# A hybrid decoder block on one core: the first half's input projection takes the input times the norm's weight alone, and the norm's factor is multiplied onto its results

## Chip, cores and metric

The kernel runs on one core of a Trainium2 chip. The metric is device time in microseconds (us): 2113.87 us, the median of three runs (2112.77 to 2115.74). A core has five engines with one instruction stream each: TensorE (PE, matrix products), VectorE (DVE), ScalarE (ACT), GpSimd (POOL) and SyncE (SP, which issues the DMAs). Each works through its own stream in order and waits on semaphores for the others.

## The reference

One layer on x of 2048 positions by 1024 features, in float32:

```python
h = rmsnorm(x, norm1_g)              # x * rsqrt(mean(x*x) + 1e-6) * g
proj = h @ w_in                      # 3088 columns
p_q, p_k, p_v, p_g, p_a, c_b, c_c, c_h = split(proj)
q, k, v = heads of p_q * 64**-0.5, p_k, p_v
log_a = log_sigmoid(p_a @ w_gate_up + b_gate) / 16
o = rmsnorm(gla_chunked(q, k, v, log_a), gla_norm_g) * silu(p_g)
u = c_c * c_h
o_conv = c_b * causal_depthwise_conv(u, conv_w)      # width 3
x = x + concat(o, o_conv) @ w_out
h2 = rmsnorm(x, norm2_g)
x = x + (silu(h2 @ w_ffn_gate) * (h2 @ w_ffn_up)) @ w_ffn_down
out = rmsnorm(x, norm_f_g)
```

The norm's factor, rsqrt(mean(x*x) + 1e-6), is one number for each position. The norm's weight g is one number for each feature.

## The kernel before

**Layout.** Features lie on the 128 partitions, positions along the free dimension. A tile is 128 features by 512 positions (256 KB). The 2048 positions are four blocks of 512; two blocks (j = 0, 1) make a half, and the input projection, the output projection and the feed-forward part run once for each half. The input comes twice: `xt` as tiles with the features on the partitions, and `x` as rows, from which the squares of the norm are summed.

**Numbers.** Products are made from float32 values that are split in two parts, a high part (an ACT copy that rounds, line 153) and the rest (a DVE subtraction, line 154). Each product of two tiles takes three matmuls: high times high, high times rest, rest times high (lines 366 to 368; in the first unit lines 297 to 299).

**Units.** The input projection of a half (`in_proj`, line 596) has twelve units of 256 columns: k, q, v, v, g, g, then twice the three of the convolution (c_c, c_h, c_b). An ordinary unit (`unit`, line 370) is a Strassen-like scheme with seven products of 12 matmuls in the place of eight. It needs sums and differences of the weight's quarters, which POOL makes (lines 349 to 356) and ACT and DVE split into a buffer of four (`wqp`), and differences T1 to T4 of the operand tiles, which POOL makes for the first half (line 310). Three of its four results end in SBUF through ACT copies and DVE additions (lines 386, 390), the fourth stays in PSUM. The first two units of the first half are plain products of eight parts (96 matmuls each): the first in `build_first` (line 273), so that it can begin before all operands are there, the second in `plain_unit` (line 315).

**The start.** `first_loads` (line 466) issues on SP's queue: four tiles of rows of block 0 (`xr`), two quarters of the first weights, four tiles of `xt`, the other two quarters, four more tiles of `xt`; then the rows and the tiles of block 1. At most eight loads are under way at a time. ACT squares and sums the rows (`row_squares`, line 463), `rows_rstd` (line 449) works out the factor in steps on 128x4 values, and DVE spreads it into `rep` tiles (line 457; two buffers), which PE transposes into a PSUM bank (line 458). `scaled` (line 489) then multiplies each tile of the input by the weight and that bank in one DVE instruction (line 490). The product goes through the split and the six matmuls of its step in the first unit. Block 1's factor follows after the first eight steps.

**Order of the work.** The instructions of each engine are put in order when the program is built, by a scheduler with a timeline of its own, and are then fixed. Work in the background runs between products: `tick` (line 201) calls a step of a list of generators, one after the other: the gate's weights (`gate_weights`, line 494), the factors of blocks 2 and 3 (`row_stats`, line 427), the forget gate of the first half (`gate`, line 547), then `h1_ahead` (line 516), which makes the second half's operands with the same `scaled` and stores them, and later the attention (`gla_half`, line 649). Results of the projection are stored to scratch in DRAM: k, q and v through `settled` (an ACT copy where they stand in PSUM, line 410), g through `silu` (line 420), the convolution's through the lines 622 to 647.

**Buffers.** Tiles `t` (nine), tiles `b` (eleven), operands `op` (28), PSUM banks (eight).

## Time and profile before

| | |
|---|---|
| median of three runs | 2113.87 us |
| profiled execution: span, first to last instruction | 2109.1 us |
| PE busy | 2033.1 us, 9133 matmuls |
| DVE busy | 1418.4 us |
| ACT busy | 1014.1 us |
| POOL busy | 972.4 us |
| moved by DMA | 464.43 MB |

The profile is of one execution. It gives the time of every instruction, what each engine waited for, and in "windows" the busy time of each engine in a stretch of the span. "x" is a count, and a mean is in ns where a row says so. The tile names in a row are the program's (`op` operand, `wq` weight quarter, `h` input tile, `mm` PSUM bank, `rep` and `rb_ps` the spread factor). One time stands beside the span for the whole run: the median, 4.8 us above the span of the profiled execution.

### The profile page before, as it was taken

Reading aid. Unit: us, or ns where it says so; the run is one execution under the profiler, and the core shown is the slowest. Engines: PE = TensorE matmul, PEld = TensorE weight load, DVE = VectorE, ACT = ScalarE, POOL = GpSimd, SP = SyncE. Lnnn points to the kernel's source line nnn. Section 1 sums busy time; section 2 is a strip of 40 time slices with the busy share of each in tenths; the row PEclk is TensorE's granted clock in tenths of the full one; section 3 lists DMA queues with packets and bytes.
Section 4 is the critical chain, followed back from the end, with each engine's and each line's share of the span. In section 5 each row is a group of like instructions: output and inputs, shape, how many; then the busy total and the mean of one; then the engine's idle time right before and its main releaser. Section 6 shows DMA issues by size and latency. Waiting matters only on the chain.

```text
span 2109.1 us, 26874 instructions
## 1 busy us (share of the span) xinstructions
PE 2033.1 (96%) x9133; PEld 1648.9 (78%) x9133; DVE 1418.4 (67%) x1983; ACT 1014.1 (48%) x1997; POOL 972.4 (46%) x703
## 2 busy tenths in 40 slices
PE   5999999999999999999999999999999989999996
PEld 4778888877888878788888878787888868877775
DVE  7669786549753786788786665554766666665564
ACT  5555455656542356445545443333554554543344
POOL 3436322222102464564464348764645544436774
PEclk9999999999999999999999999999999999999998
DMA  7349485425586872656545687697454535587763
GB/s 277 126 158 318 139 329 164 148 83 164 201 284 235 325 249 100 241 198 221 217 172 220 243 327 272 235 338 296 158 207 179 206 134 190 183 344 281 269 269 110
DMA packets 189241, 464.43 MB, mean 220 GB/s; under 512 B 19824, under 2 KB 65072, under 8 KB 179504
## 3 DMA queue, kind: packets, MB, share of 16 engines
q1 hardware_dynamic: 189104, 462.72, 60.4%
q8 instruction: 72, 1.18, 0.2%
q14 instruction: 65, 0.53, 0.1%
HBM read 297.49 MB, written 165.15 MB: 219 GB/s over the span
## 4 chain that ended last, share of the span: by engine, by line
PE 70%; DVE 8%; DMA 7%; ACT 3%; issue 3%; POOL 2%; SPq 0%; DVEq 0%; ACTq 0%; POOLq 0%
PE mm L366 21%; PE mm L368 21%; PE mm L367 21%; DVE wq L154 2%; DMA op<-shT 1%; DVE so L154 1%; PE mm L794 1%; DVE h L490 1%; PE mm L795 1%; PE mm L797 1%; DVE op L154 1%; DMA sx<-y 1%; ACT wq L153 1%; PE o_ps L718 1%; DMA shT<-so 1%
## 5 line engine op out<-in xcount | busy, mean ns | idle before, releaser
L366 PE MATMUL mm<-op,wq 128*128 128x512 f32 x2499 | 981.3, 395 | 23.8 <-DVE c L390 7.8
L368 PE MATMUL mm<-op,wq 128*128 128x512 f32 x2499 | 966.1, 392 | 12.6 <-DVE wq L154 11.9
L367 PE MATMUL mm<-op,wq 128*128 128x512 f32 x2499 | 976.0, 391 | 0.0
L154 DVE TENSOR_TENSOR wq<-raw,wq 128x512 fp32r<-128x512 f32 (+2 forms) x626 | 527.3, 849 | 329.9 <-ACT wq L153 324.3
L153 ACT ACTIVATE wq<-raw 128x512 fp32r<-128x512 f32 (+2 forms) x626 | 363.6, 587 | 555.8 <-PE mm L368 402.4
L366 PEld LDWEIGHTS mm<-op,wq 128*128 128x128 f32 x2499 | 470.8, 188 | 137.6 <-ACT wq L153 12.3
L368 PEld LDWEIGHTS mm<-op,wq 128*128 128x128 f32 x2499 | 470.5, 188 | 123.5 <-DVE wq L154 24.8
L367 PEld LDWEIGHTS mm<-op,wq 128*128 128x128 f32 x2499 | 471.2, 189 | 96.7 <-issue 1.0
L351 POOL TENSOR_TENSOR raw<-s,raw 128x512 f32<-128x512 f32 (+2 forms) x97 | 127.5, 1314 | 422.2 <-DVE wq L154 402.0
L390 DVE TENSOR_TENSOR c<-mm,c 128x512 f32<-128x512 f32 x267 | 183.0, 686 | 95.7 <-PE mm L368 93.0
L349 POOL TENSOR_TENSOR s<-raw 128x512 f32<-128x512 f32 (+2 forms) x97 | 130.2, 1343 | 216.2 <-DMA raw<-in_wffn_dram 88.8
L356 POOL TENSOR_TENSOR raw<-raw 128x512 f32<-128x512 f32 (+2 forms) x97 | 126.7, 1306 | 135.3 <-DVE wq L154 128.1
L386 ACT ACTIVATE c<-mm 128x512 f32<-128x512 f32 x267 | 154.7, 585 | 38.0 <-PE mm L368 36.8
L776 POOL TENSOR_TENSOR ssx<-ssx,q 128x512 f32<-128x512 f32 x52 | 76.5, 1483 | 156.0 <-ACT q L775 155.8
L350 POOL TENSOR_TENSOR raw<-raw 128x512 f32<-128x512 f32 (+2 forms) x97 | 135.1, 1393 | 4.1
L965 POOL TENSOR_TENSOR y<-c,y 128x512 f32<-128x512 f32 x66 | 98.7, 1499 | 49.0 <-DVE c L390 46.6
L154 DVE TENSOR_TENSOR so<-t,so 128x512 fp32r<-128x512 f32 x100 | 91.2, 918 | 25.9 <-ACT so L153 25.4
L153 ACT ACTIVATE wq<-s 128x512 fp32r<-128x512 f32 (+2 forms) x97 | 56.9, 586 | 93.5 <-PE mm L368 83.3
L794 PE MATMUL mm<-op,wq 128*128 128x512 f32 x256 | 100.9, 395 | 0.0
L795 PE MATMUL mm<-op,wq 128*128 128x512 f32 x256 | 99.8, 390 | 0.0
L154 DVE TENSOR_TENSOR wq<-s,wq 128x512 fp32r<-128x512 f32 (+2 forms) x97 | 84.1, 867 | 15.6 <-ACT wq L153 15.0
L153 ACT ACTIVATE so<-t 128x512 fp32r<-128x512 f32 x100 | 62.5, 627 | 41.8 <-DMA sa_T<-so 16.1
(177 smaller groups left out, 1885.0 us busy)
## 6 DMA issues: line engine op xcount, KB each, us to landing
raw<-in_wffn_dram SPq DMA_DIRECT2D x44, 1024.0 KB, 5.7
sa_T<-so SPq DMA_DIRECT2D x88, 512.0 KB, 5.3
op<-sa_T SPq DMA_DIRECT2D x88, 512.0 KB, 9.2
sa_B<-so SPq DMA_DIRECT2D x69, 512.0 KB, 3.4
op<-sa_B SPq DMA_DIRECT2D x69, 512.0 KB, 9.0
raw<-in_win_dram SPq DMA_DIRECT2D x23, 1024.0 KB, 5.5
raw<-in_wdown_dram SPq DMA_DIRECT2D x24, 768.0 KB, 6.2
sx<-y SPq DMA_DIRECT2D x48, 256.0 KB, 3.2
```

Source lines behind the costliest of these rows:

```text
L153: last_hi[:] = [act.activation(hi, src, AF.Copy)]
L154: return dve.tensor_tensor(lo, src, hi.bitcast(F32), ALU.subtract)
L349: pool.tensor_tensor(s1, a21, a22, ALU.add)
L350: pool.tensor_tensor(a21, a11, a21, ALU.subtract)
L351: pool.tensor_tensor(a11, s1, a11, ALU.subtract)
L356: pool.tensor_tensor(a12, a12, a11, ALU.subtract)
L366: pe.matmul(o[:], wh, xh, start=first and k == 0, stop=False, skip_group_check=True)
L367: pe.matmul(o[:], wh, xl, start=False, stop=False, skip_group_check=True)
L368: return pe.matmul(o[:], wl, xh, start=False, stop=k == n - 1, skip_group_check=True)
L386: act.activation(t[:], o[:], AF.Copy)
L390: dve.tensor_tensor(t[:], o[:], t[:], ALU.add)
L794: pe.matmul(o[e, j][:], wh, m[:, 0, :], start=k == 0, stop=False)
```

## The change

The first half's operands are now the input times the weight g; the factor of the position is left out of them. Since the factor belongs to a position, and positions are columns of every result, it can be multiplied onto the results.

- **Loads.** `first_loads` issues the first weights and the 16 tiles of `xt` first, then the second unit's weights, then all eight tiles of rows. Five of the `xt` tiles lie in tiles `t`, eleven in tiles `b` (before: eight and eight).
- **Operands.** For each tile ACT makes the high part straight from the input with g as its scale, DVE makes the rest in one instruction (input times g less the high part; both tensors in SBUF), and POOL multiplies the tile itself by g in place, for the differences T1 to T4. The 16 instructions of line 490 on DVE and the 16 splits behind them become 16 on DVE and 16 on POOL.
- **Factor.** The squares, the two factors and their transposes come after the first unit in the program's text. ACT copies each factor from PSUM to SBUF (`factors`), and for the results c_c its square (`factors2`).
- **Results.** `factored` multiplies a result by the factor: on POOL where it stands in SBUF, on DVE where it stands in PSUM (which takes the place of the ACT copy). It runs on k, q, v, g and c_c; c_h and c_b have none, since c_c takes the square for both itself and c_h, and the convolution's result is multiplied by the factor once more on POOL for c_b. The forget gate multiplies its 16 rows on DVE on the way out of PSUM.
- The first unit's four results are copied out of PSUM by ACT at once. The waits set by hand (`issue_after` on `los`, on `last_load`) are gone.

The second half, its operands (`h1_ahead`) and all that follows are as before.

```diff
@@ -270,25 +270,23 @@
             put("B22", k, b22)
             yield
 
-    def build_first(quad, w):
+    def build_first(h, w):
 
 
         ops = {b: [] for _, b in PRODUCTS}
-        h, o = {}, {}
+        o, out = {}, []
         quarters = ("A11", "A12"), ("A21", "A22")
-        los = []
         for j in range(2):
             for r in range(2):
                 o[r, j] = bank()
             for k in range(KD):
-                with ExitStack() as stack:
-                    if len(los) > 1:
-                        stack.enter_context(tc.issue_after(los[-2].ins))
-                    h[k, j] = quad(k, j)
+                g = col(C_G1 + k)
                 x = opp.tile([P, 2, PB], F32R, name="op", tag="op")
-                los.append(split(h[k, j][:], x[:, 0, :], x[:, 1, :]))
-                if j == 0 and k >= PT:
-                    row_squares(1, k - PT)
+                act.activation(x[:, 0, :], h[k, j][:], AF.Copy, scale=g)
+                dve.scalar_tensor_tensor(
+                    x[:, 1, :], h[k, j][:], g, x[:, 0, :].bitcast(F32), ALU.mult, ALU.subtract
+                )
+                pool.tensor_scalar(h[k, j][:], h[k, j][:], g, 1.0, ALU.mult, ALU.mult)
                 name = ("B11", "B12")[j] if k < 4 else ("B21", "B22")[j]
                 ops.setdefault(name, []).append(x)
                 c = slice(k % 4 * P, (k % 4 + 1) * P)
@@ -297,8 +295,15 @@
                     pe.matmul(o[r, j][:], q[:, 0, c], x[:, 0, :], start=k == 0, stop=False)
                     pe.matmul(o[r, j][:], q[:, 0, c], x[:, 1, :], start=False, stop=False)
                     pe.matmul(o[r, j][:], q[:, 1, c], x[:, 0, :], start=False, stop=k == KD - 1)
-            if j == 0:
-                rbs[1] = rows_rstd(squares[1])
+            for r in range(2):
+                c = tt("c")
+                act.activation(c[:], o[r, j][:], AF.Copy)
+                out.append((r, j, c, False))
+        for b in range(2):
+            for t in range(PT):
+                row_squares(b, t)
+            factors[b] = tiny.tile([P, PB], F32, name="rb", tag="rb")
+            act.activation(factors[b][:], rows_rstd(squares[b])[:], AF.Copy)
 
         def differences(wanted):
             for n, y, a, b in (
@@ -310,11 +315,10 @@
                     pool.tensor_tensor(yy[:], aa[:], bb[:], ALU.subtract)
                     ops[n].append(split_op(yy[:]))
 
-        return ops, [(r, j, o[r, j], True) for j in range(2) for r in range(2)], differences
-
-    def plain_unit(src, ops):
-
-        raw = raw_weights(src)
+        return ops, out, differences
+
+    def plain_unit(raw, ops):
+
         us, columns = [], (("B11", "B21"), ("B12", "B22"))
         for r, row in enumerate(((0, 1), (3, 2))):
             w = [weight_quarter(raw[:, i, :]) for i in row]
@@ -324,7 +328,7 @@
                     for k in range(4):
                         product_step(o, w[i], ops[n], k, i == 0)
                     tick()
-                us.append((r, j, settled(o, True), False))
+                us.append((r, j, o, True))
         return us
 
     def weight_quarter(src):
@@ -458,7 +462,7 @@
             pe.transpose(rb_ps[:, t * P : (t + 1) * P], rep[:], ident[:])
         return rb_ps
 
-    rbs, raws, first_weights, last_load, rows, squares = {}, {}, {}, [], {}, {}
+    rbs, raws, first_weights, rows, squares, factors, factors2 = {}, {}, {}, {}, {}, {}, {}
 
     def row_squares(b, t):
         act.activation(rows[b, t], rows[b, t], AF.Square, accum_out=squares[b][:, t, 0:1])
@@ -466,6 +470,16 @@
     def first_loads():
 
         raw = rawp.tile([P, 4, PB], F32, name="raw", tag="raw")
+        for j in range(2):
+            for k in range(KD):
+                if j == 0 and k % 4 == 0:
+                    for i in ((0, 3), (1, 2))[k // 4]:
+                        raw_loads.append(load(raw[:, i, :], win[0][:, i, :]))
+                h = raws[k, j] = bt("h") if len(raws) > 4 else tt("h")
+                load(h[:], xt[j, :, k, :])
+        for n, i in (("A11", 0), ("A21", 3), ("A12", 1), ("A22", 2)):
+            first_weights[n] = weight_quarter(raw[:, i, :])
+        second = raw_weights(win[1])
         for b in range(2):
             squares[b] = mtiny.tile([P, PT, 2], F32, name="ssq", tag="ssq")
             for t in range(PT):
@@ -473,18 +487,7 @@
                 rows[b, t] = xr[:]
                 r0 = b * PB + t * P
                 load(xr[:], x[r0 : r0 + P, :])
-            for k in range(KD):
-                if b == 0 and k % 4 == 0:
-                    for i in ((0, 3), (1, 2))[k // 4]:
-                        raw_loads.append(load(raw[:, i, :], win[0][:, i, :]))
-                h = bt("h") if b else tt("h")
-                raws[b, k] = h
-                last_load[:] = [load(h[:], xt[b, :, k, :])]
-        for t in range(PT):
-            row_squares(0, t)
-        rbs[0] = rows_rstd(squares[0])
-        for n, i in (("A11", 0), ("A21", 3), ("A12", 1), ("A22", 2)):
-            first_weights[n] = weight_quarter(raw[:, i, :])
+        return second
 
     def scaled(g, rb, h):
         dve.scalar_tensor_tensor(h[:], h[:], g, rb[:], ALU.mult, ALU.mult)
@@ -505,13 +508,11 @@
         split(r1, low[:, :, 2, :], low[:, :, 3, :])
         yield
 
-    def build_h():
-
-
-        def quad(k, j):
-            return scaled(col(C_G1 + k), rbs[j], raws[j, k])
-
-        return build_first(quad, first_weights)
+    def factored(c, in_psum, f):
+
+        s = tt("n") if in_psum else c
+        (dve if in_psum else pool).tensor_tensor(s[:], c[:], f[:], ALU.mult)
+        return s
 
     def h1_ahead():
 
@@ -560,7 +561,12 @@
                         stop=n == "B22" and k == 3 and e == 1, skip_group_check=True,
                     )
         a_sb = bt("a_sb")
-        act.activation(a_sb[:], a[:], AF.Copy)
+        if half:
+            act.activation(a_sb[:], a[:], AF.Copy)
+        else:
+            for j in range(2):
+                r = slice(32 * j, 32 * j + 32)
+                dve.tensor_tensor(a_sb[r, :], a[r, :], factors[j][r, :], ALU.mult)
         yield
         for j in range(2):
             small = decays[2 * half + j] = [
@@ -593,16 +599,20 @@
         dve.tensor_tensor(dn[:, i, :], em[:, i, :], el[:, i, :], ALU.mult)
         store(s_d[b][i][:], t2[:])
 
-    def in_proj(half, ops, first=None, differences=None):
+    def in_proj(half, ops, first=None, second=None, differences=None):
+        def values(u):
+            f = factors2 if u in (6, 9) else factors
+            for r, j, c, p in next(units):
+                if half == 0 and u not in (7, 8, 10, 11):
+                    c, p = factored(c, p, f[j]), False
+                yield r, j, c, p
+
         def units():
             for u in range(12):
-                with ExitStack() as stack:
-                    if half == 0 and u == 1:
-                        stack.enter_context(tc.issue_after(last_load[0].ins))
-                    if half or u > 1:
-                        us = unit(win[u], ops)
-                    else:
-                        us = plain_unit(win[u], ops) if u else first
+                if half or u > 1:
+                    us = unit(win[u], ops)
+                else:
+                    us = plain_unit(second, ops) if u else first
                 if half == 0 and u == 1:
                     del ops["B12"]
                     differences(("T4",))
@@ -611,16 +621,21 @@
         units = units()
         if half == 0:
             differences(("T1", "T2", "T3"))
-        for dst, i0 in ((s_kq, 0), (s_kq, 2), (s_v, 0), (s_v, 2)):
-            for r, j, c, p in next(units):
+        for u, (dst, i0) in enumerate(((s_kq, 0), (s_kq, 2), (s_v, 0), (s_v, 2))):
+            for r, j, c, p in values(u):
                 store(dst[2 * half + j][i0 + r][:], settled(c, p)[:])
         for i0 in (0, 2):
-            for r, j, c, p in next(units):
+            for r, j, c, p in values(4 + i0 // 2):
                 store(s_g[2 * half + j][i0 + r][:], silu(c, p)[:])
         background.append(gla_half(half))
+        if half == 0:
+            for j in range(2):
+                factors2[j] = tiny.tile([P, PB], F32, name=f"rr{j}", tag=f"ssx{j}", bufs=1)
+                act.activation(factors2[j][:], factors[j][:], AF.Square)
         for i0 in (0, 2):
-            cc = {(r, j): settled(c, p) for r, j, c, p in next(units)}
-            ch = {(r, j): c for r, j, c, _ in next(units)}
+            u = 6 + 3 * (i0 // 2)
+            cc = {(r, j): settled(c, p) for r, j, c, p in values(u)}
+            ch = {(r, j): c for r, j, c, _ in values(u + 1)}
             for r in range(2):
                 i = i0 + r
                 left = halo[:, i, :]
@@ -635,9 +650,11 @@
                         dve.scalar_tensor_tensor(
                             y[:], s[:, n : n + PB], col(C_CW + 4 * n + i), y[:], ALU.mult, ALU.add
                         )
+                    if half == 0:
+                        pool.tensor_tensor(y[:], y[:], factors[j][:], ALU.mult)
                 if half == 0:
                     act.activation(halo[:, i, :], left, AF.Copy)
-            for r, j, c, _ in next(units):
+            for r, j, c, _ in values(u + 2):
                 y = cc[r, j]
                 dve.tensor_tensor(y[:], c[:], y[:], ALU.mult)
                 hi = tp.tile([P, PB], F32R, name="hi", tag="t")
@@ -1047,10 +1064,10 @@
 
 
     act.preload_act_table_set("natural_log_exp_and_others")
-    first_loads()
+    second = first_loads()
     for i in range(4):
         load(wgu_sb[16 * i : 16 * i + 16, :], wgu[0:16, :])
-    ops, first, differences = build_h()
+    ops, first, differences = build_first(raws, first_weights)
     hurry.append(True)
     background.extend(
         [
@@ -1058,7 +1075,7 @@
             h1_ahead(),
         ]
     )
-    in_proj(0, ops, first, differences)
+    in_proj(0, ops, first, second, differences)
     drain_background(lambda: len(background) < 2)
     ops = load_pairs(s_h1)
     background.append(gate(1, ops))
```

## The prediction

> **What bounds the kernel now.** I read the page first (busy shares, chain of waits), then PE's own waits in the first 320 us, then the stretches there.
>
> ```profile
> span 2109.1 us, 26874 instructions
> ...
> PE 2033.1 (96%) x9133; PEld 1648.9 (78%) x9133; DVE 1418.4 (67%) x1983; ACT 1014.1 (48%) x1997; POOL 972.4 (46%) x703
> ...
> PE 70%; DVE 8%; DMA 7%; ACT 3%; issue 3%; POOL 2%; SPq 0%; DVEq 0%; ACTq 0%; POOLq 0%
> ```
>
> PE is busy 96% of the span, and 70% of the chain is PE. The change adds no matmul and takes none away, so it can pay only where PE stands still or runs slowly.
>
> ```profile
> PE rb_ps L458 <- DVE rep L457: 14.3, 2, 14.1
> PE mm L368 <- DVE wq L154: 4.2, 2, 2.1
> ```
>
> ```profile
> 0.00:17.83 17.83, 1.35 (x5) 0.66 (x5) 7.12 (x21) 9.05 (x17) 1.11 (x7) 1.00 0.86 300
> 17.83:24.02 6.19, 6.19 (x16) 4.58 (x17) 5.71 (x10) 4.60 (x9) 0.00 (x0) 1.00 1.01 395
> 24.02:33.00 8.98, 8.33 (x38) 6.56 (x36) 5.37 (x15) 4.28 (x10) 0.00 (x0) 1.00 0.99 349
> 33.00:70.00 37.00, 29.50 (x111) 22.02 (x112) 36.86 (x43) 26.14 (x66) 27.77 (x18) 0.92 0.53 186
> 80.00:140.00 60.00, 60.00 (x256) 46.44 (x255) 27.16 (x54) 24.47 (x46) 11.62 (x9) 1.00 0.27 95
> 160.00:220.00 60.00, 59.40 (x260) 48.65 (x261) 56.90 (x66) 31.61 (x62) 38.26 (x25) 1.00 0.88 297
> ```
>
> Columns after the length: busy time of PE, weight loads, DVE, ACT, POOL, then clock, DMA share, GB/s. Nothing useful runs on PE before 17.83 us. From 33 to 70 us DVE is full (36.86 of 37.00) and PE idles 7.5 us. From 80 to 140 PE is full and DVE and POOL are half empty. From 160 to 220 us, while the second half's operands are made (`h1_ahead`), PE is just full and DVE nearly so.
>
> **What the change does to the first matmul.** Before, it waits for the rows, their squares, the factor and its transposes. After, it waits for eight transfers of 256 KB (2 MB: all of the first weights and four tiles of the input), four weight splits and one ACT copy.
>
> ```profile
> 4.88 1.06 ACT L464 ACTIVATE xr<-xr 128x1024 f32<-128x1024 f32 x1 [2.80 <-DMA xr<-in_x_dram]
> ...
> 9.59 1.06 ACT L464 ACTIVATE xr<-xr 128x1024 f32<-128x1024 f32 x1
> ...
> 17.16 1.13 ACT L153 ACTIVATE op<-h 128x512 fp32r<-128x512 f32 x2
> ```
>
> ```profile
> 17.83 1.22 PE L297 MATMUL mm<-op,wq 128*128 128x512 f32 x2 [2.30 <-ACT op L153]
> ...
> 19.85 0.63 PE L298 MATMUL mm<-op,wq 128*128 128x512 f32 x1
> 20.28 0.63 PE L299 MATMUL mm<-op,wq 128*128 128x512 f32 x1
> ...
> 24.02 0.39 PE L299 MATMUL mm<-op,wq 128*128 128x512 f32 x1
> 24.24 0.39 PE L298 MATMUL mm<-op,wq 128*128 128x512 f32 x1
> ```
>
> Today the first 2 MB are four tiles of rows, squared as they land; the last square starts at 9.6 us. So the last weight quarter lands at about 9.6; its copy and the first operand's follow at ACT's pitch of about 0.5 (two in 1.13): first matmul at 10.7 us, against 17.83. The first dozen go at 0.43 us apart, later ones at 0.227, so the 96 matmuls of the first unit take 96 x 0.227 = 21.8 plus 12 x 0.2 = 2.4 and end at 34.9 us. ACT (16 copies, 8.3 us) and the 12 further input tiles (3 MB, at 300 to 395 GB/s some 9 us) keep ahead of them.
>
> **What stands behind it.** In the changed program's instruction order PE has five transposes next, before any matmul of the second unit: four for the factor of block 0 and one for block 1. That fifth reads the first `rep` copy of block 1, and DVE has 25 instructions between the last of the 16 new splits and that copy: 10 large splits (six difference operands, four weight quarters), three splits of `wa`, eight 128x4 steps of the two factors, four `rep` copies. PE's order is fixed, so the second unit waits for all of them. POOL meanwhile has 16 new products of input and weight, and up to that point 16 tensor-by-tensor operations (14 differences, two weight sums). So the question is how DVE and POOL run side by side.
>
> ```profile
> 188.60 0.68 DVE L154 TENSOR_TENSOR lo<-t,hi 128x512 fp32r<-128x512 f32 x1
> 189.20 0.68 DVE L154 TENSOR_TENSOR lo<-h,hi 128x512 fp32r<-128x512 f32 x1
> ...
> 193.22 1.78 DVE L154 TENSOR_TENSOR lo<-h,hi 128x512 fp32r<-128x512 f32 x1
> ```
>
> ```profile
> 186.84 1.29 POOL L351 TENSOR_TENSOR raw<-s,raw 128x512 f32<-128x512 f32 x1
> ...
> 191.00 1.75 POOL L349 TENSOR_TENSOR s<-raw 128x512 f32<-128x512 f32 x1
> ```
>
> ```profile
> 57.53 1.24 DVE L452 TENSOR_SCALAR msq<-ssq 128x4 f32<-128x4 f32 x1
> ...
> 62.39 0.16 DVE L165 SCALAR_TENSOR_TENSOR msq<-rl,ry 128x4 f32<-128x4 f32 x1
> ```
>
> Two DVE splits alone start 0.60 apart; a POOL operation alone takes 1.29. Next to each other a split takes up to 1.78 and the POOL operation up to 1.75: they take turns, and a split's turn is 1.78 - 1.29 = 0.48. Even a 128x4 step waits its turn (1.24 against 0.16). The old product, line 490, has an operand in PSUM and keeps its time beside POOL:
>
> ```profile
> L490 DVE SCALAR_TENSOR_TENSOR h<-h,sml,rb_ps 128x512 f32<-128x512 f32 x11 | 8.1, 736 | 0.0
> L390 DVE TENSOR_TENSOR c<-mm,c 128x512 f32<-128x512 f32 x9 | 6.1, 679 | 0.0
> ...
> L629 DVE TENSOR_TENSOR u<-mm,c 128x512 f32<-128x512 f32 x1 | 0.7, 678 | 0.0
> ```
>
> That is 160 to 220 us, grouped: all three read PSUM and their means stay near the 0.68 of a free operation. The new split with the weight has both tensors in SBUF, and a POOL product follows it.
>
> POOL's new product with one input has no row. The nearest one-input rows are these:
>
> ```profile
> 1.08 0.29 POOL masks.py:199 TENSOR_SCALAR_AFFINE_SELECT ident<-ident 128x128 f32<-128x128 f32 x1
> 1.40 0.41 POOL L80 TENSOR_SCALAR_AFFINE_SELECT mask<-mask 128x256 f32<-128x256 f32 x1
> ```
>
> 0.12 us for 128 more elements makes 0.64 for 512 (an estimate). The other end is 1.29, as for two inputs; below, nothing excludes that it is hidden. I take 0.64, the nearer operation. The Trainium skill's GPSIMD Engine Reference (4.1 Engine selection) calls one-input work there about line rate, and 3.1 gives 1.03 cycles an element, which makes an estimate of 0.44 us; by that the sum below would come out 16 x 0.2 = 3.2 us lower. Its 8. Key points say that GpSimd contends with DVE instructions that have two SBUF inputs; the trace agrees, 1.78 against 0.68.
>
> Taking turns from 11.0 us (first weight splits done): 16 new DVE splits x 0.48 = 7.7; 16 POOL products x 0.64 = 10.2; 16 POOL operations x 1.29 = 20.6; 10 large DVE splits x 0.48 = 4.8; 15 small ones at about 0.1 = 1.5. Sum 44.8, so the copy is done at 55.8 us. PE has then stood still for 55.8 - 34.9 = 20.9 us and starts slowly again.
>
> ```profile
> L458 PE MATMUL rb_ps<-ident,rep 128*128 128x128 f32 x16 | 3.9, 319 | 14.4 <-DVE rep L457 14.3
> ```
>
> The second unit's 96 matmuls take 21.8, slow start 2.4, three more transposes in between 3 x 0.32 = 1.0: the third unit starts at 55.8 + 25.2 = 81.0 us. Today:
>
> ```profile
> 81.00 0.63 ACT L153 ACTIVATE wq<-raw 128x512 fp32r<-128x512 f32 x1 [1.60 <-PE mm L368]
> ...
> 83.78 0.63 ACT L153 ACTIVATE wq<-raw 128x512 fp32r<-128x512 f32 x1 [1.66 <-PE mm L368]
> ```
>
> These weight copies wait for PE to free a buffer, one product (12 matmuls, 2.7 us) apart. The first product of the third unit ended at 80.95, so it began at 78.1. The early start is thus lost: **+2.9 us**. By then DVE has caught up, and the third unit's weights (24 more DVE instructions, about 25 us) come before PE asks for them.
>
> **The factor on the results.** The first unit gets four POOL products of two inputs, the second four DVE products from PSUM, six later units three on POOL and one on DVE; the convolution gets eight more on POOL. The DVE products need no turn, and most take the place of an ACT copy. The third to the fifth unit hide theirs: POOL is busy 11.6 of 60 us from 80 to 140. From 160 to 220 the turns are nearly all taken: 66 DVE instructions less the 21 from PSUM above are 45 x 0.48 = 21.6; 25 POOL operations x 1.29 = 32.3; together 53.9 of 60 us. The changed order has eight more POOL products there (three units), 10.3 us: 64.2 for 60. Ends: 0, if the background slips into the emptier time behind, and 11.3, if the turns are used only to today's 90% (64.2 / 0.9 - 60). I take **+3.5**, a little under the 4.2 of the sum, for the weight buffers that PE has in hand. Behind this stage PE's order of instructions is the same in both programs, and the products on the convolution have only a late store behind them: nothing.
>
> **Sum.** +2.9 + 3.5 = +6.4 us. The profiled execution's span is 2109.1, 4.8 us under the median of 2113.87; what lies around the span stays, so 2113.87 + 6.4 = **2120 us**. A measurement of this kernel can tell about 0.2% (4.2 us) from no change.
>
> **The rivals.**
> - DVE gets ahead of POOL. The turns bind only while both always have work; where POOL waits for a difference's split, DVE runs free. At the far end nothing is held: the eighth row tile lands at about 32 us (10.5 MB at the rates of the first three stretches), is squared by 34, and 20 DVE instructions remain, seven large at 0.60 and 13 small at 0.17: 41 us instead of 55.8. With 3.5 behind, 2120.3 - 14.8 = 2105.5, faster. For it: POOL idles 9.2 of 37 us from 33 to 70. Against: DVE was full there all the same. It decides at 53 us: an earlier copy is a gain at the start. Chance 0.17.
> - `h1_ahead` hides the factor: only +2.9, 2116.8, within 0.2%. For it: PE lost only 0.6 us there. Against: the turns' sum of 64.2. Chance 0.2.
> - POOL's one-input product takes the 1.29 of two inputs: 16 x 0.65 = 10.4 more ahead of the copy, 2131, slower. The trace has no such row. Chance 0.15.
> - The change doesn't start PE earlier: the 2 MB would have to land after 16 us; the row at 9.59 speaks against it, so I give it nothing.
>
> **How the numbers follow.** Forecast 0.48, rivals 0.17, 0.2, 0.15. Faster by over 0.2%: 0.17; within: the second rival and the low edge of the forecast's own spread, 0.23; slower: 0.60. The range goes from the first rival to the third: 2105 to 2131.
>
> **What would show it.** First matmul at 10.7 us; the 96 without a long wait, ending near 35; then the longest wait of PE: a transpose behind a DVE `rep` copy, some 20 us, followed by slow matmuls; DVE splits of 1.1 to 1.8 beside POOL from 11 to 55 us; third unit at 81; PE waits on DVE weight splits between 160 and 220. A wait of PE under 15 us, or POOL's new product far from 0.64, would make the prediction wrong.

## The result, and the profile after

| | before | after |
|---|---|---|
| median | 2113.32 us (4 runs) | 2128.45 us (4 runs, 2126.58 to 2130.71) |
| ratio, 95% interval | 1 | 1.0078 [1.0059, 1.0097] |
| span of the profiled execution | 2109.1 us | 2124.7 us |

The changed kernel is slower by 15.1 us. The ratio is an estimate from the single runs, not the quotient of the two medians (1.0072). The forecast was 2120 with a range of 2105 to 2131: side and range held, but the loss is more than twice the 6.4 us that the sum gave.

The page of the changed kernel, first the engines' busy times and then the chain of work that ended last:

```profile
PE 2035.5 (96%) x9133; PEld 1649.8 (78%) x9133; DVE 1439.1 (68%) x1979; ACT 1013.1 (48%) x1992; POOL 1037.0 (49%) x749
...
PE 77%; DVE 9%; DMA 6%; ACT 3%; issue 3%; POOL 2%; SPq 0%; DVEq 0%; ACTq 0%; POOLq 0%
```

PE has the same 9133 matmuls. POOL has 64.6 us more, DVE 20.7 us; PE's share of the chain goes from 70% to 77%.

Where the 15 us come from is read best from one kind of instruction that both kernels have in the same order: the ACT copies of PE's partial products to SBUF (line 386 before, 390 after). PE's progress sets them. The same four copies, first before, then after (start in us, duration):

```profile
81.54 0.58 ACT L386 ACTIVATE c<-mm 128x512 f32<-128x512 f32 x1
...
139.39 0.58 ACT L386 ACTIVATE c<-mm 128x512 f32<-128x512 f32 x1
...
255.68 0.60 ACT L386 ACTIVATE c<-mm 128x512 f32<-128x512 f32 x1
...
324.34 0.58 ACT L386 ACTIVATE c<-mm 128x512 f32<-128x512 f32 x1
```

```profile
85.90 0.58 ACT L390 ACTIVATE c<-mm 128x512 f32<-128x512 f32 x1
...
143.76 0.58 ACT L390 ACTIVATE c<-mm 128x512 f32<-128x512 f32 x1
...
271.58 0.59 ACT L390 ACTIVATE c<-mm 128x512 f32<-128x512 f32 x1
...
340.70 0.58 ACT L390 ACTIVATE c<-mm 128x512 f32<-128x512 f32 x1
```

The changed kernel is 4.4 us late in the third unit and still 4.4 late at 140 us; at 256 us it is 15.9 late, at 324 us 16.4. The spans end 15.6 apart. So there are two places: **the start costs 4.4 us, the stretch from 140 to 260 us costs 12**, and the remaining 1850 us cost nothing. The 12 us build up step by step: in the five units that follow, the last of these copies comes 7.5, 9.0, 13.8, 14.3 and 16.4 us late (at 171, 192, 216, 236 and 257 us).

The start, in PE's timeline after (start, duration; in brackets the idle time before and what ended it), and then DVE's:

```profile
12.74 1.22 PE L295 MATMUL mm<-op,wq 128*128 128x512 f32 x2 [12.74 <-ACT op L285]
...
48.27 0.45 PE L462 MATMUL rb_ps<-ident,rep 128*128 128x128 f32 x1 [11.32 <-DVE rep L461]
...
58.53 0.47 PE L462 MATMUL rb_ps<-ident,rep 128*128 128x128 f32 x1 [4.17 <-DVE rep L461]
58.66 0.77 PE L370 MATMUL mm<-op,wq 128*128 128x512 f32 x1
```

```profile
12.73 17.53 DVE L286 SCALAR_TENSOR_TENSOR op<-h,sml,op 128x512 fp32r<-128x512 f32 x16
...
57.19 1.42 DVE L461 COPY rep<-msq 128x128 f32<-128x128 f32 x2
```

The first unit's matmuls run from 12.74 to 36.96 without a wait. Then PE's next instructions are five transposes, each waits for a `rep` copy, and the second unit's first matmul comes right behind the fifth one, at 58.66. PE's waits, grouped (us in all, times, longest), say the same:

```profile
PE rb_ps L462 <- DVE rep L461: 19.7, 5, 11.3
```

The stretches from 80 us on (columns as in the prediction), and what PE waited for, first here from 140 to 262 us, then in the kernel before over the same units (136 to 246 us):

```profile
80.00:140.00 60.00, 60.00 (x256) 46.46 (x255) 30.96 (x54) 21.39 (x38) 22.11 (x15) 1.00 0.25 84
140.00:160.00 20.00, 17.62 (x71) 13.75 (x71) 20.00 (x31) 12.59 (x24) 10.79 (x8) 0.93 0.74 246
160.00:220.00 60.00, 55.42 (x233) 42.80 (x232) 57.76 (x59) 28.54 (x53) 47.82 (x31) 0.99 0.80 271
```

```profile
PE mm L372 <- DVE wq L154: 6.3, 10, 2.0
PE mm L370 <- ACT c L390: 3.9, 3, 2.1
```

```profile
PE mm L368 <- DVE wq L154: 2.1, 1, 2.1
PE mm L366 <- ACT c L386: 0.9, 1, 0.9
```

From 80 to 140 us POOL's new products fit beside a full PE. From 140 to 262 us PE stands 10.2 us in many small waits (6.3 us in ten on DVE's weight splits, 3.9 in three on ACT's copies), against 3.0 us before. So 7.2 of the 12 us are added waits; the clock, 0.93 of full from 140 to 160 us, is worth 1.4 more (an estimate, 0.07 of 20 us), and the rest is not assigned. DVE is full until 220 us (20.00 of 20.00, then 57.76 of 60), but so it was before (20.00 and 56.90); what is new from 160 to 220 us is POOL's load, 47.82 us for 38.26.

The waits for ACT's copies have another source than the weight splits. The longest (2.1 us) ends with the copy at 232.28, and what stands just ahead of that copy in ACT's order has waited for a load:

```profile
231.95 0.42 ACT L698 ACTIVATE ee<-ee 128x256 f32<-128x256 f32 x1 [4.19 <-DMA ee<-sd]
232.28 0.58 ACT L390 ACTIVATE c<-mm 128x512 f32<-128x512 f32 x1
```

The next longest (1.3 us) ends with the copy at 215.51, behind ACT's wait of 2.47 us for a POOL difference at 214.46.

### The profile page after: what moved, and what is told of

It is laid out like the page before. It is cut to its first block, busy times and chain, and to the rows that moved or that the text cites. A ratio compares the mean times of both kernels' runs of the same rounds, so it can differ in the third digit from the quotient of the medians.

```text
span 2124.7 us, 26941 instructions
## 1 busy us (share of the span) xinstructions
PE 2035.5 (96%) x9133; PEld 1649.8 (78%) x9133; DVE 1439.1 (68%) x1979; ACT 1013.1 (48%) x1992; POOL 1037.0 (49%) x749
## 4 chain that ended last, share of the span: by engine, by line
PE 77%; DVE 9%; DMA 6%; ACT 3%; issue 3%; POOL 2%; SPq 0%; DVEq 0%; ACTq 0%; POOLq 0%
PE mm L370 22%; PE mm L372 22%; PE mm L371 21%; PE mm L811 3%; PE mm L812 3%; PE mm L814 3%; DVE wq L154 3%; DVE so L154 1%; DMA op<-shT 1%; DMA raw<-in_wffn_dram 1%; DMA h<-in_xt_dram 1%; PE a_ps L559 1%; DVE h L493 1%; DVE c L394 1%; PE o_ps L735 1%
## 5 line engine op out<-in xcount | busy, mean ns | idle before, releaser
L372 PE MATMUL mm<-op,wq 128*128 128x512 f32 x2499 | 967.1, 393 | 14.8 <-DVE wq L154 14.3
L370 PEld LDWEIGHTS mm<-op,wq 128*128 128x128 f32 x2499 | 471.4, 189 | 139.4 <-ACT wq L153 12.7
```

The costliest lines, as they stand in the source:

```text
L370: pe.matmul(o[:], wh, xh, start=first and k == 0, stop=False, skip_group_check=True)
L372: return pe.matmul(o[:], wl, xh, start=False, stop=k == n - 1, skip_group_check=True)
```

## The experiments

Two theories go with the two places. **At the start**: PE's fixed order (the five transposes ahead of the second unit) gives the early start away, while DVE and POOL take turns. **From 140 us**: the factor's products on POOL take turns from DVE's splits. Against them stand: the sum of DVE's and POOL's work, and not an order, holds the start; and the late loss is one of the compiler's order, not of the products. Each kernel below is the changed kernel with the edit shown. Ratios are to the kernel before, measured in the same series; the changed kernel stands at 1.0078.

### 1. No late factor

The units from the third on keep their results without the factor; its squares (`factors2`), which nothing reads then, go too.

```diff
-                if half == 0 and u not in (7, 8, 10, 11):
+                if half == 0 and u < 2:
...
-                    if half == 0:
-                        pool.tensor_tensor(y[:], y[:], factors[j][:], ALU.mult)
```

> This kernel leaves out part of the computation: units 3 to 12 of the first half and the convolution keep their results without the norm's factor (the first two units keep theirs). Theory (turns): the +12 us between 145 and 262 us come from the 8 to 14 factor products that POOL gets there and from the turns they take from DVE's splits; without them the time falls from 2128.4 by about 12 us, to 2116 (2113 to 2119), and the copies from PSUM of the third unit stay where they are (first near 85.9 us). Rival (order): the loss comes from the compiler's other order and the later start of the whole, not from the products; then it stays at 2126 to 2129.

Measured 2117.84 us, ratio 1.0020 [1.0009, 1.0030]. Two of its copies:

```profile
144.12 0.58 ACT L390 ACTIVATE c<-mm 128x512 f32<-128x512 f32 x1
...
329.08 0.58 ACT L390 ACTIVATE c<-mm 128x512 f32<-128x512 f32 x1
```

It is 4.7 us late at 144 us, and still 4.7 late at 329: the late loss is gone to the last tenth, and the start's is untouched. The products (POOL's and DVE's together) cause all of the 12 us; the rival falls. How they cause it, the run does not tell.

### 2. The factor's products on DVE

```diff
-        (dve if in_psum else pool).tensor_tensor(s[:], c[:], f[:], ALU.mult)
+        dve.tensor_tensor(s[:], c[:], f[:], ALU.mult)
...
-                        pool.tensor_tensor(y[:], y[:], factors[j][:], ALU.mult)
+                        dve.tensor_tensor(y[:], y[:], factors[j][:], ALU.mult)
```

> All factor products stand on DVE instead of POOL. Theory (turns): a product on DVE takes one turn of 0.48 to 0.6 us instead of one of 1.29 on POOL, so 8 to 14 of them cost 5 to 8 us instead of 12: 2121 (2118 to 2125). Rival (DVE is full from 160 to 220 us, 57 of 60 us, so whatever is given to it comes on top): 14 x 0.68 = 9.5 us more on the fuller engine and nothing back from POOL, 2128 to 2134.

Measured 2126.18 us, 1.0060 [1.0038, 1.0082]: the intervals overlap with the change's, and no late gain shows. Its stretch, and the products that replace POOL's from 140 to 262 us (count, busy us, mean ns):

```profile
160.00:220.00 60.00, 56.70 (x235) 44.21 (x233) 59.55 (x68) 28.61 (x53) 36.66 (x25) 0.97 0.85 289
...
L514 DVE TENSOR_TENSOR c<-c,rb 128x512 f32<-128x512 f32 x6 | 8.1, 1348 | 0.0
L514 DVE TENSOR_TENSOR c<-c,rr 128x512 f32<-128x512 f32 x6 | 5.2, 863 | 0.0
```

POOL is relieved (36.66 for 47.82), DVE goes from 57.76 to 59.55 of 60. A product in SBUF takes DVE 0.86 to 1.35 us, about the 1.1 us that a product on POOL costs PE here (12 us over eleven). The idea that it would need a cheap turn of 0.48 there falls: the splits and the product are all on the one full engine. PE's timeline separates the two places: at 300 us PE is 12.0 us behind the kernel before, but at the third unit's start only 0.9 (79.00 us; the change 82.44, the kernel before 78.08). So the late loss is 11.1 for 12.0, and the start is 3.5 us better. There the fifth transpose comes at 55.04 instead of 58.53. Everything is 1.4 us earlier (the first transpose at 46.91 for 48.27); the other 2.1 fall where POOL, in the changed kernel, runs two products of the first unit's results from 55.07 on, beside the `rep` copy. The profile ends as late as the change's all the same (2124.7): after 300 us PE's lag moves by a few us in every profile, in the change's own from 16.4 down to 11.6 and up to 15.2.

### 3. The factors behind the second unit

```diff
             for t in range(PT):
                 row_squares(b, t)
+
+        def make_factors():
+          for b in range(2):
             factors[b] = tiny.tile([P, PB], F32, name="rb", tag="rb")
             act.activation(factors[b][:], rows_rstd(squares[b])[:], AF.Copy)
...
             differences(("T1", "T2", "T3"))
+            two = [next(units), next(units)]
+            make_factors()
+            units = chain(two, units)
```

> The two factors (their 128x4 steps, the copies rep and the eight transposes) are written behind the second unit, so PE's order has no transpose ahead of its matmuls. Theory (PE's order of instructions loses the early start): the second unit starts near 42 us instead of 58.7 and the third near 70 us instead of 82.7; 12 us less in all, 2116 (2113 to 2120). Rival (DVE and POOL together are the bound, whatever PE's order is): the second unit starts early but waits inside itself and before the third unit for DVE's splits, the third unit starts at 80 to 83 us, and the time is 2126 to 2130.

Measured 2128.12 us, 1.0068 [1.0047, 1.0088]: no gain. PE's timeline (the transposes have line 465 here) and ACT's:

```profile
37.77 0.50 PE L373 MATMUL mm<-op,wq 128*128 128x512 f32 x1 [1.38 <-ACT wq L153]
...
62.84 0.38 PE L465 MATMUL rb_ps<-ident,rep 128*128 128x128 f32 x2
73.54 0.69 PE L465 MATMUL rb_ps<-ident,rep 128*128 128x128 f32 x2 [10.32 <-DVE rep L464]
```

```profile
68.91 0.63 ACT L451 ACTIVATE xn<-xn 128x512 f32<-128x512 f32 x1
...
69.53 2.17 ACT L153 ACTIVATE op<-h 128x512 fp32r<-128x512 f32 x4
```

The second unit starts at 37.8 us instead of 58.7: DVE and POOL can deliver that early. But the wait has only moved. `rep` has two buffers, so the third copy waits for PE to read the first; in DVE's order it then stands behind the splits of T4, those behind ACT's copies `op<-h`, and these behind 16 squares of the next block's rows (`xn`). The third unit waits for the third transpose until 73.5. Neither expectation fits: the time is the rival's, the mechanism is an order.

So the next kernel frees the transposes: one `rep` tile of 128x512 for each block, and the squares of the next rows behind the last T4 split.

```diff
-            act.activation(factors[b][:], rows_rstd(squares[b])[:], AF.Copy)
+            act.activation(factors[b][:], rows_rstd(squares[b], tiny.tile([P, PB], F32, name="rep", tag=f"ssx{b}", bufs=1))[:], AF.Copy)
...
-                act.activation(xn[:], xn[:], AF.Square, accum_out=ssq[:, t, e : e + 1])
+                with tc.issue_after(last_split[-1].ins):
+                    act.activation(xn[:], xn[:], AF.Square, accum_out=ssq[:, t, e : e + 1])
```

> The factors stand behind the second unit as in the run before, and two things are freed: the copies rep have one tile of 128x512 for each block (no two-buffer wait on PE's transposes), and the row squares of block 2 stand behind the last T4 split on ACT. Theory (the early start is lost by what PE's order of instructions has to wait for, not by the sum of DVE's and POOL's work): the transposes find their copies ready when the second unit ends near 63 us, the third unit starts at 64 to 66 us instead of 82.7, and the first half as a whole gains 12 to 17 us: 2113 (2110 to 2117). Rival (DVE and POOL cannot deliver earlier): the third unit's weights come after 72 us, the waits of PE move into the third unit, and the time is 2124 to 2128.

Measured 2117.54 us, 1.0018 [1.0008, 1.0028], some 12 us less than the change. PE's timeline, and two of ACT's copies:

```profile
64.21 1.03 PE L470 MATMUL rb_ps<-ident,rep 128*128 128x128 f32 x8
65.00 0.48 PE L374 MATMUL mm<-op,wq 128*128 128x512 f32 x1
```

```profile
131.85 0.58 ACT L394 ACTIVATE c<-mm 128x512 f32<-128x512 f32 x1
...
328.95 0.58 ACT L394 ACTIVATE c<-mm 128x512 f32<-128x512 f32 x1
```

All eight transposes run in one go, and the third unit starts at 65.0, as expected, 17.4 us earlier than in the changed kernel. Not all of it lasts: 5.4 us are given back within the third unit (the fourth starts at 89.71 for 101.75), where PE waits 0.9 us for ACT's copy of the factor and 2.2 us for ACT's copy of a result. At 131.85 it is 7.5 us ahead of the kernel before (139.39). The start's loss is thus mostly one of order: the same products, splits and differences stand ahead, and only what PE, DVE and ACT have to pass first has changed. At 329 us, behind the products, it is 4.6 us late again: 12.1 us, the same late loss.

### 4. Both terms at once

The kernel above without the late factor (the edit of the first run).

> The run with the factors behind the second unit and freed, and in addition the factor is left out of the units 3 to 12 of the first half and of the convolution (part of the computation is left out, as in the first run). Theory (start and late products are two separate terms that add): 2117.5 - 11 = 2106 to 2108, which is the change with its early start kept and its factor free, 6 to 8 us below the kernel before. Rival (the earlier start is given back where the second half's operands are made, whatever the products do): 2111 to 2115.

Measured 2105.06 us, 0.9963 [0.9951, 0.9975], and the copy at 316.06 instead of 324.34, 8.3 us ahead. The terms add: 1.0018 less the first run's 0.0058 would be 0.9960. This is what the change would be worth if the factor cost nothing and the transposes stood where their data is ready.

### 5. The products of input and weight: on ACT, or not at all

```diff
-                pool.tensor_scalar(h[k, j][:], h[k, j][:], g, 1.0, ALU.mult, ALU.mult)
+                act.activation(h[k, j][:], h[k, j][:], AF.Copy, scale=g)
```

> The 16 products of input and weight for the difference operands stand on ACT instead of POOL. Theory (turns): 16 x 0.68 = 10.9 us of POOL's turns go, the fifth rep copy comes at 47 us instead of 57.6 and the third unit starts near 72 us instead of 82.7: 2118 (2115 to 2121). Rival (POOL's differences and DVE's splits alternate by their data, so POOL's products fill gaps that are there anyway): 3 us or less, 2125 to 2129.

Measured 2133.07 us, 1.0089 [1.0071, 1.0107]; no gain, against the theory. The stretch from 12.7 to 36 us:

```profile
12.70:36.00 23.30, 23.30 (x94) 19.01 (x93) 10.14 (x16) 23.30 (x40) 9.17 (x8) 1.00 0.92 359
```

ACT is now full (23.30 of 23.30), POOL nearly idle (9.17), and the row squares, which the factor waits for, come late. The run says nothing of POOL's turns. So the next one leaves the line out:

> This kernel leaves out part of the computation: the 16 products of the input with the norm's weight on POOL (the difference operands T1 to T4 are then made of the bare input); all else is as in the changed kernel, PE's order too. Theory (turns): 16 x 0.68 = 10.9 us of POOL work go from the stretch between 12 and 57 us, the DVE splits beside them fall from 1.10 to about 0.6, the fifth rep copy comes at 45 to 48 us and the third unit 9 to 12 us earlier: 2117 (2115 to 2121). Rival (the differences and their splits wait for each other anyway): at most 3 us, 2125 to 2128.

Measured 2127.81 us, 1.0069 [1.0051, 1.0087], the fifth transpose at 57.77 instead of 58.53. The DVE splits from 12.7 to 57 us, first of the changed kernel, then of this one:

```profile
L286 DVE SCALAR_TENSOR_TENSOR op<-h,sml,op 128x512 fp32r<-128x512 f32 x16 | 17.5, 1168 | 0.0
...
L154 DVE TENSOR_TENSOR op<-h,op 128x512 fp32r<-128x512 f32 x6 | 5.0, 828 | 3.9 <-ACT op L153 3.9
```

```profile
L286 DVE SCALAR_TENSOR_TENSOR op<-h,sml,op 128x512 fp32r<-128x512 f32 x16 | 19.0, 1262 | 0.0
...
L154 DVE TENSOR_TENSOR op<-h,op 128x512 fp32r<-128x512 f32 x12 | 12.1, 1037 | 2.2 <-ACT op L153 2.1
```

16 POOL products, 17.6 us of busy time, are gone and the copy comes as late as ever. The differences move up to the place of the products, and beside them a split takes longer (1.26 for 1.17 us); and the compiler's order now has twelve difference splits ahead of the copy instead of six, and sixteen differences instead of fourteen. The number is the rival's. Since the order changed with the edit, the run shows neither that the rival's reason holds nor what the products alone cost.

### 6. The convolution's products alone

```diff
-                    if half == 0:
-                        pool.tensor_tensor(y[:], y[:], factors[j][:], ALU.mult)
```

> This kernel leaves out part of the computation: the eight products of the convolution with the factor; the products on the units' results stay. As the prediction has it (only a late store stands behind them): no change, 2127 to 2130. Rival (they take turns from the weight splits between 215 and 262 us): 8 x 0.48 = 3.8 us less, 2124 to 2125.

Measured 2129.11 us, 1.0076 [1.0058, 1.0093]. No change: the 12 us belong to the products on the units' results.

### 7. The second half's operands earlier, or spread

Three runs move what the products collide with. First, `pause(9)` becomes `pause(0)`.

> The pause of nine steps ahead of the second half's row sums is gone, so that the making of the second half's operands starts nine steps (about 24 us) earlier, in the stretch where DVE is half empty. Theory (the products cost 12 us only because they fall where DVE and POOL are full): the loss between 140 and 262 us shrinks from 12 to 4 to 8 us: 2122 (2119 to 2125). Rival (each product costs wherever the second half's operands are made): 2126 to 2131, with the waits of PE on weight splits moved to 115 to 235 us; the row squares, now beside the second unit, could also cost 1 to 3 us there.

Measured 2132.26 us, 1.0089 [1.0069, 1.0109]: the rival's side, just above its range, and no gain. Then the DVE product of each input tile of the second half is put behind the last sum of the unit in hand, so that these products are spread to about 290 us:

```diff
-            return scaled(col(g + k), rb[j], h)
+            with ExitStack() as stack:
+                if last_plus and g == C_G1:
+                    stack.enter_context(tc.issue_after(last_plus[0].ins))
+                return scaled(col(g + k), rb[j], h)
```

> The changed kernel with only the second half's DVE products spread as above (factors where the change has them). Theory (full stretch): 12 us of loss become 2 to 6, so 2128.4 - 8 = 2120 (2117 to 2123); the start stays as it is, first copies of the third unit near 86 us. Rival: no gain, 2126 to 2131.

Measured 2148.25 us, 1.0171 [1.0151, 1.0190].

```profile
140.00:210.00 70.00, 69.63 (x307) 57.31 (x307) 57.56 (x75) 36.05 (x67) 47.48 (x31) 1.00 0.63 212
210.00:330.00 120.00, 97.45 (x413) 78.11 (x412) 88.78 (x106) 43.66 (x85) 64.26 (x38) 0.90 0.65 229
```

Up to 210 us the loss is gone: PE is busy 69.63 of 70 us, with the products in place and DVE at 57.56 of 70. The theory holds there. But the operands now collide with the convolution and the first steps of `gla_half`, and PE loses 22.5 of the next 120 us (the kernel before: nothing, 119.99). The same edit on the freed kernel:

> The run with the factors behind the second unit and freed (2117.5), and in addition the second half's DVE products stand behind the last sum of the unit in hand, so that the compiler's order spreads them from 140 to about 290 us instead of 140 to 222. Theory (each late POOL product costs its whole 1.29 us only where DVE has no free time): the loss between 140 and 262 us shrinks from 12 to 2 to 6 us and the time is 2108 (2105 to 2112), below both kernels. Rival (the products cost wherever they stand, or the later operands hold up the second half's start): 2115 to 2122.

Measured 2134.93 us, 1.0112 [1.0093, 1.0130], by the same two readings (PE 48.67 of 50 us from 160 to 210, then 96.30 of 120). Moving the operands is no cure.

### 8. Fewer products in the full stretch

The freed kernel, with the order of units 0, 1, 4, 5, 2, 3, 6 to 11, and v's factor on ACT's copy of its transpose:

```diff
-                if half == 0 and u not in (7, 8, 10, 11):
+                if half == 0 and u not in (2, 3, 7, 8, 10, 11):
...
-        act.activation(v[:], v_ps[:], AF.Copy)
+        if b < 2:
+            act.activation(v[:], v_ps[:], AF.Copy, scale=tokens[b][:, t : t + 1])
+        else:
+            act.activation(v[:], v_ps[:], AF.Copy)
```

> The run with the factors behind the second unit and freed (2117.5), and the units of g (which need their factor before the silu) stand ahead of the units of v; v takes its factor later, on the copy of its transpose on ACT, where the tokens are the partitions and the factor is a scale of an instruction that is there anyway. Six products of POOL and two of DVE go, those of the units that stand in the full stretch from 140 to 180 us. Theory (10 POOL products there cost 12 us): about 6 of 10 go, so 5 to 8 us: 2111 (2109 to 2114), level with the kernel before or just below it. Rival (the stretch is full whatever is taken out, or the other order of units costs elsewhere): 2116 to 2120.

Measured 2114.29 us, 1.0014 [1.0002, 1.0026]. By the medians that is 3.3 us less than the freed kernel, by the ratios 0.8, and the expected gain was 5 to 8. It is not below the kernel before, and the ratio's interval takes in the freed kernel's 1.0018. Its copies at 174 and 201 us, and what ACT does between:

```profile
174.36 0.60 ACT L394 ACTIVATE c<-mm 128x512 f32<-128x512 f32 x1
...
194.31 0.63 ACT L153 ACTIVATE hi<-t 128x512 fp32r<-128x512 f32 x1 [7.02 <-POOL t L254]
...
195.36 1.06 ACT L394 ACTIVATE c<-mm 128x512 f32<-128x512 f32 x2
...
201.51 0.60 ACT L394 ACTIVATE c<-mm 128x512 f32<-128x512 f32 x1 [2.27 <-PE mm L376]
```

At 174.36 it has no late loss at all: the freed kernel without a late factor (section 4) has this copy at 174.63. One unit later it is 7.8 us behind that run (201.51 against 193.67). ACT waits 7.02 us for a POOL difference of the second half; the copies that PE needs stand behind that wait. PE stands 3.2 us for them, and right behind that its granted clock is 0.51 of full from 195 to 202 us, worth some 3.4 us more (an estimate, 0.49 of 7 us). So what six products fewer had won was lost again within one unit, through another queue. That this chain is the cause there is read from the rows, not tested.

## Why the prediction was right, point by point

- **First matmul at 10.7 us: 12.74.** Two us late. The last two weight quarters reach ACT at 10.8, and the copy of the first operand ends at 12.7; I had let the 2 MB land at 9.6, the rate at which the rows landed before.
- **96 matmuls without a wait, ending at 34.9: 36.96.** The length is right (24.2 us for 24.2), and it starts 2 us later.
- **PE's order then holds the second unit behind the fifth transpose.** Right: 21.7 us from 36.96 to 58.66, of them 19.7 on `rep` copies, and the slow matmuls behind it. The freed kernel shows that it is the order: its third unit starts at 65.0.
- **The copy done at 55.8 by a sum of turns: at 58.4** (the two in 1.42 from 57.19, the second one 0.21). The size was right; the sum as a mechanism is not shown. It left out two factor products on POOL (3.32 us at 55.07), and it began at 11.0 us where the first of the 16 splits came at 12.73. Without the 16 products, 10.2 us of the 44.8, the transpose moves by 0.8 us; by the sum, six more splits (2.9) and two more differences (2.6) ahead of the copy should have left a gain of 4.7. Which instruction stands ahead of the copy in DVE's order is decided again in each program.
- **POOL's one-input product: 0.64 estimated.** Alone it takes 0.68 (two in 1.36), beside DVE's splits 1.1. The Trainium skill's GPSIMD Engine Reference (3.1), with 1.03 cycles an element, gave 0.44 as an estimate; the measurement decides against it here.

```profile
13.58 11.63 POOL L289 TENSOR_SCALAR h<-h,sml 128x512 f32<-128x512 f32 x10 [11.77 <-DVE op L286]
...
34.42 1.36 POOL L289 TENSOR_SCALAR h<-h,sml 128x512 f32<-128x512 f32 x2
```

- **Start +2.9: +4.4.** The copy is 2.6 us later than forecast, and from it to the third unit it takes 1.1 us less than the 25.2. The late first matmul counts in it: in three runs whose programs have the same start, the second unit begins 45.8 to 45.9 us after the first matmul, whether that one comes at 12.05 (the spread operands), 12.24 (no late factor) or 12.74 us (the change).
- **The products from 160 to 220 us +3.5: +12.** This is the step that failed, as a size: "I take +3.5, a little under the 4.2 of the sum, for the weight buffers that PE has in hand." The sum gave the new products the 6 us of turns that were free on paper. The runs show no such cover: with the products, PE loses 12.0 to 12.2 us (first run; freed kernel with and without them), a little over the far end of 11.3 that I had worked out for turns used only to today's 90%. The place was right: the product that the kernel before starts at 160.60 comes 5.0 us late, the one at 218.18 comes 14.7 late, so 9.7 of the 12 us fall in the stretch that the term was for (+3.5). The other 2.3 fall on either side, where I had put nothing. Nor was the count too low: from 140 to 262 us POOL has eleven of these products, and six of them start between 160 and 220 us, where I had counted eight:

```profile
L514 POOL TENSOR_TENSOR c<-c,rb 128x512 f32<-128x512 f32 x6 | 9.9, 1655 | 4.1 <-DVE c L394 4.1
L514 POOL TENSOR_TENSOR c<-c,rr 128x512 f32<-128x512 f32 x5 | 7.7, 1550 | 5.9 <-DVE c L394 5.9
```

The waits of PE on weight splits from 160 us on came as foretold, but they are small and many, and 3.9 of PE's 10.2 us of waits are for ACT's copies, which the sum of DVE's and POOL's turns has no term for.
- **The convolution's products cost nothing.** Right (1.0076).
- **Rivals.** The copy at 41 us didn't come, and `h1_ahead` didn't hide the factor. The one with the dearer product had the nearest time, 2131, for the wrong reason.

The answer fell inside the range because its upper edge, set by another rival, covered the size of the late loss; that was luck. That the products cause the late loss is shown; how it divides between DVE's turns, ACT's order and the clock is read from the rows and not tested. What stays open too is why six products fewer in the full stretch (the last run) bring so little; the wait of ACT for POOL is the nearest reading.

## What to carry to other kernels

Moving a factor from the operands to the results turns work in front of the matmuls into work behind them; ask in which stretch the results fall, and if an engine is 95% busy there, charge each new operation its full length, with no credit for the slots that look free. Here DVE was that engine, and eleven products of 1.29 us each when alone, 14.2 us, cost 12; the eight of the convolution, half of them behind 262 us, cost nothing. Look also at what else stands in the order of an engine that PE waits for: a copy that is ready can stand behind a wait for something else. An earlier first matmul is worth only as much as the next thing in PE's order allows: list what stands between it and the first later wait, and put transposes behind work whose data is there, with buffers enough that their inputs are made ahead. Here three edits of the products themselves (the factor's on DVE, the weight's on ACT or left out) gained nothing that can be told from the change, and one edit of the order gained 12 us.

## What the runs showed of the hardware

- In the changed kernel a DVE operation in SBUF takes longer beside POOL even when it is small: copies of 128x128 took 1.27 us each (two in 2.53 at 46.82) beside POOL's two-input operations, and 0.21 alone (at 59.14), where both read and write SBUF.

```profile
46.82 2.53 DVE L461 COPY rep<-msq 128x128 f32<-128x128 f32 x2
...
59.14 0.21 DVE L461 COPY rep<-msq 128x128 f32<-128x128 f32 x1
```

- The DVE operations that read PSUM keep their length beside POOL: in the changed kernel from 160 to 220 us the sums of line 394 take 676 ns, the weight splits, with both operands in SBUF, 1267.

```profile
L154 DVE TENSOR_TENSOR wq<-raw,wq 128x512 fp32r<-128x512 f32 x17 | 21.3, 1267 | 0.5 <-ACT wq L153 0.5
...
L394 DVE TENSOR_TENSOR c<-mm,c 128x512 f32<-128x512 f32 x8 | 5.4, 676 | 0.0
```
